# One store for five groups, and a last group in 12 KB runs: a batched matmul on one core

## The chip, the core and the metric

The kernel runs on one core of a Trainium2 chip. The core has a matrix engine (PE, with its weight loads PEld), a vector engine (DVE), a scalar engine (ACT), POOL, which does nothing here, and SP, which issues the transfers. All transfers between the chip's DRAM and the on-chip buffers run on 16 DMA engines, and one transfer is spread over all 16. The metric is device time in microseconds (us). The kernel before takes 134.25 us, the median of four runs (134.11 to 134.53).

## The reference

```
x: (32, 256, 512) float32      y: (32, 512, 384) float32
out = einsum('bij,bjk->bik', x, y)  as float32
```

There are 32 independent products of a 256x512 matrix with a 512x384 one. Inputs are 41.94 MB, outputs 12.58 MB.

## The kernel before

Four batches make a group, so there are eight groups, 0 to 7. A group's x, y and outputs lie on all 128 partitions, 32 partitions for each of its four batches. For x, a partition holds eight rows of 512 (16 KB, one run in DRAM); for y, sixteen rows of 384 (24 KB, one run). The outputs of a group take 12 KB per partition, eight rows of 384.

Each group goes through steps, each named by a letter with the group's number. `x` and `y` are the loads (lines 89 and 98). `T` casts x to float16 and transposes it in blocks of 32 by 32 on DVE (lines 108 and 115). `R` casts y to float16 on DVE (line 121). `M` is 128 matmuls (line 140): first the 64 of half `e` = 0, then the 64 of `e` = 1; within a half, four row strips of the matrix engine work for the four batches `g`. Each pair `(e, g)` has a bank of PSUM, the matmuls' output memory, and these are all eight banks. `C` and `D` copy the banks to the output tile (line 161): `C` is ACT's share and `D` DVE's, chosen by `on_vector`. `S` stores a group's output tile (line 168).

The order of the work is written out by hand in the string `PLAN`; each engine, and SP for the transfers, keeps that order. The stores of groups 0 to 4 stand after the last load, `y7`. Those of groups 5, 6 and 7 stand at the end.

How the rows of a group are dealt to partitions is decided by `width(n)`. For groups 0 to 5 it is 32: a copy moves 32 partitions by 384, a bank takes four copies, and a partition ends with eight consecutive rows of the output, one run of 12,288 B in DRAM. For groups 6 and 7 it is 64: a copy moves 64 partitions, a bank takes two, and a partition ends with two runs of 6,144 B that are 786,432 B apart in DRAM. `width` is used in the transpose, the copies and the store, which must agree.

Of the copies, DVE takes the last bank of groups 0 to 5, none of group 6, and the odd `g` of group 7; ACT takes the rest. So of the 16 copies of group 7 each of the two takes eight.

Buffers: x and y have two each. The output pool has five, for groups 0 to 4. Groups 5 and 6 put their outputs into x buffers that have been read; group 7 takes an output buffer again, the one that group 0 used, and so comes after store 0.

Of the kernel before, what the change touches and what calls it, by code (L numbers as in the profile page):

```python
# [1 line left out]

# [4 lines left out]


MM_DT = mybir.dt.float16
F32 = mybir.dt.float32  # L10
P = 128


Q = 4
STEP = 4
O_BUFS = 5
WIDE_GROUPS = 6

O_IN_X = (5, 6)

PLAN = """
y0 x0 y1 x1
R0 T0 M0 C0 x2 y2
R1 T1 D0 M1 C1 x3
T2 D1 R2 M2 C2 x4 y3
T3 D2 R3 M3 C3 x5 y4
T4 D3 R4 M4 C4 x6 y5  # L30
T5 x7 y6 D4 R5 T6 M5 C5 y7 S0 S1 S2 S3 S4
D5 R6 T7 M6 C6
R7 M7 C7 D7 S5 S6 S7
"""


@with_exitstack
def kernel(
    ctx: ExitStack,
    tc: tile.TileContext,  # L40
    x: bass.AP,
    y: bass.AP,
    out: bass.AP,
):
    nc = tc.nc

    B, I, J = x.shape
    _, _, K = y.shape

    PQ = P // Q  # L50
    R = I // PQ
    T = J // PQ
    TW = T // 2
    NE = I // P
    N = B // Q

    x_pool = ctx.enter_context(tc.tile_pool(name="x_pool", bufs=2))
    y_pool = ctx.enter_context(tc.tile_pool(name="y_pool", bufs=2))
    xr_pool = ctx.enter_context(tc.tile_pool(name="xr_pool", bufs=1))
    xt_pool = ctx.enter_context(tc.tile_pool(name="xt_pool", bufs=3))  # L60
    yr_pool = ctx.enter_context(tc.tile_pool(name="yr_pool", bufs=2))
    o_pool = ctx.enter_context(tc.tile_pool(name="o_pool", bufs=O_BUFS))
    psum_pool = ctx.enter_context(
        tc.tile_pool(name="psum", bufs=1, space=bass.MemoryType.PSUM)
    )

    keep = tc.keep_in_program_order

    bank = {
        (e, g): psum_pool.tile([P, K], F32, name=f"o_ps_{e}_{g}") for e in range(NE) for g in range(Q)  # L70
    }

    x_of, y_of, xt_of, yr_of, ps_of, o_of = {}, {}, {}, {}, {}, {}

    def width(n):
        return PQ if n < WIDE_GROUPS else 2 * PQ

    def on_vector(n, e, g):
        if n < WIDE_GROUPS:
            return (e, g) == (NE - 1, Q - 1)
        return n == N - 1 and g % 2 == 1

    def load_x(n):
        x_of[n] = x_pool.tile([P, R, J], F32, name="x_sb")
        keep(
            nc.sync.dma_start(
                out=x_of[n],  # L90
                in_=x[n * Q : (n + 1) * Q].rearrange("g (p r) j -> (g p) r j", r=R),
            )
        )

    def load_y(n):
        y_of[n] = y_pool.tile([P, T, K], F32, name="y_sb")
        keep(
            nc.sync.dma_start(  # L98
                out=y_of[n],
                in_=y[n * Q : (n + 1) * Q].rearrange("g (q t) k -> (g q) t k", t=T),  # L100
            )
        )

    def transpose_x(n):


        x_r = xr_pool.tile([P, R, J], MM_DT, name="x_r")
        keep(nc.vector.tensor_copy(x_r, x_of.pop(n)))  # L108
        xt_of[n] = xt_pool.tile([P, NE, TW, P], F32, name="xt_sb")
        b = width(n) // PQ  # L110
        src = x_r.bitcast(F32).rearrange("p (b h e) (q t) -> p b e t h q", b=b, e=NE, t=TW)
        dst = xt_of[n].rearrange("p e t (h s b) -> p b e t h s", s=PQ, b=b)
        for e in range(NE):
            for c in range(b):
                keep(nc.vector.transpose(dst[:, c, e], src[:, c, e]))  # L115

    def round_y(n):
        y_sb = y_of.pop(n)
        yr_of[n] = yr_pool.tile([P, T, K], MM_DT, name="y_r")
        for a in range(0, T, STEP):  # L120
            keep(nc.vector.tensor_copy(yr_of[n][:, a : a + STEP], y_sb[:, a : a + STEP]))  # L121

    def multiply(n):
        xt = xt_of.pop(n).bitcast(MM_DT).rearrange("p e t (m c) -> p e t m c", c=2)
        y_r = yr_of.pop(n)
        if n in O_IN_X:
            x_sb = x_pool.tile([P, R, J], F32, name="x_sb")
            o_of[n] = x_sb.rearrange("p r j -> p (r j)")[:, : R * K].rearrange(
                "p (r k) -> p r k", r=R
            )  # L130
        else:
            o_of[n] = o_pool.tile([P, R, K], F32, name="o_sb")
        for e in range(NE):
            for g in range(Q):
                ps_of[n, e, g] = bank[e, g]
            for t in range(T):
                for g in range(Q):
                    s = slice(g * PQ, (g + 1) * PQ)
                    keep(
                        nc.tensor.matmul(  # L140
                            ps_of[n, e, g],
                            xt[s, e, t // 2, :, t % 2],
                            y_r[s, t],
                            start=(t == 0),
                            stop=(t == T - 1),
                        )
                    )

    def collect(n, vector):
        w = width(n)  # L150
        per = P // w
        copy = nc.vector.tensor_copy if vector else nc.scalar.copy
        o = o_of[n].rearrange("p (u f) k -> p u f k", u=Q // per)
        for e in range(NE):
            for g in range(Q):
                if on_vector(n, e, g) != vector:
                    continue
                ps = ps_of.pop((n, e, g))
                a = g % per * w
                for h in range(per):  # L160
                    keep(copy(o[a : a + w, g // per, h * NE + e], ps[h * w : (h + 1) * w]))  # L161

    def store(n):
        w = width(n)
        per = P // w
        dst = out[n * Q : (n + 1) * Q].rearrange("(u g) (s f) k -> (g s) u f k", g=per, s=w)
        keep(
            nc.sync.dma_start(
                out=dst, in_=o_of.pop(n).rearrange("p (u f) k -> p u f k", u=Q // per)
            )  # L170
        )

    parts = {
        "x": load_x,
        "y": load_y,
        "T": transpose_x,
        "R": round_y,
        "M": multiply,
        "C": lambda n: collect(n, False),
        "D": lambda n: collect(n, True),  # L180
        "S": store,
    }
    for step in PLAN.split():
        parts[step[0]](int(step[1:]))


# [1 line left out]
_INS = ['x', 'y']  # L188
_OUTS = [((32, 256, 384), 'float32')]


# [23 lines left out]
```

## Time and profile before

| what | us |
|---|---|
| median of four runs | 134.25 |
| the profiled execution, its own time | 134.11 |
| its span, first to last instruction | 132.3 |
| DVE busy | 95.8 |
| ACT busy | 91.5 |
| PE busy | 58.9 |
| DMA queue q1, share of 16 engines' span | 97.2% |
| a copy on ACT, 32x384 / 64x384 | 0.469 / 0.473 |
| a copy on DVE, 32x384 / 64x384 | 0.556 / 0.556 |

A page of the profile shows one execution. Its second part cuts the span into 40 equal slices; a digit is the busy share of an engine in a slice in tenths (9 is 90% or more), and the DMA row is the mean busy share of the 16 DMA engines. The timeline lists instructions in order of time: start, length, engine, line, operation, output and input, count, and in brackets the idle time before and what ended it. A table of stretches gives, for each window, the busy time of each engine, the clock granted to the matrix engine, the DMA share and the rate in GB/s. The trace also keeps a record of every DMA packet (start, length, size) and the moment at which each of the 16 engines reports that its part of a transfer has landed; durations of packets and landings of single stores are read from these.

### The profile page before, as it was taken

Reading aid. Unit: us, or ns where it says so; the run is one execution under the profiler, and the core shown is the slowest. Engines: PE = TensorE matmul, PEld = TensorE weight load, DVE = VectorE, ACT = ScalarE, POOL = GpSimd, SP = SyncE. Lnnn points to the kernel's source line nnn. Section 1 sums busy time; section 2 is a strip of 40 time slices with the busy share of each in tenths; the row PEclk is TensorE's granted clock in tenths of the full one; section 3 lists DMA queues with packets and bytes.
Section 4 is the critical chain, followed back from the end, with each engine's and each line's share of the span. In section 5 each row is a group of like instructions: output and inputs, shape, how many; then the busy total and the mean of one; then the engine's idle time right before and its main releaser. Section 6 shows DMA issues by size and latency. Waiting matters only on the chain.

```text
span 132.3 us, 2431 instructions
## 1 busy us (share of the span) xinstructions
PE 58.9 (44%) x1024; PEld 33.3 (25%) x1024; DVE 95.8 (72%) x92; ACT 91.5 (69%) x193; POOL 0.2 (0%) x4
## 2 busy tenths in 40 slices
PE   0000008951956095708581668067705867750000
PEld 0000004420534043404350335033502454430000
DVE  0007696959999999879979995999699997642000
ACT  3000000299999999999999999999999999970000
POOL 0000000000000000000000000000000000000000
PEclk9999999999599959995899689977997799998555
DMA  5999999999999999999999999999999999999993
GB/s 134 446 416 421 458 416 419 446 421 448 438 406 426 421 441 436 419 411 463 409 421 431 443 423 409 421 456 438 409 443 386 431 430 414 435 421 427 409 425 165
DMA packets 3723, 54.68 MB, mean 413 GB/s; under 512 B 384, under 2 KB 384, under 8 KB 896
## 3 DMA queue, kind: packets, MB, share of 16 engines
q1 hardware_dynamic: 3712, 54.53, 97.2%
q8 instruction: 8, 0.13, 0.4%
q14 instruction: 3, 0.02, 0.0%
HBM read 41.94 MB, written 12.58 MB: 412 GB/s over the span
## 4 chain that ended last, share of the span: by engine, by line
ACT 63%; DMA 11%; PE 8%; DVE 4%; issue 3%; DVEq 1%; SPq 0%; ACTq 0%
ACT o_sb L161 49%; ACT x_sb L161 14%; DMA x_sb<-in_x_dram 11%; PE o_ps L140 8%; DVE x_r L108 2%; DVE xt_sb L115 2%; DVE o_sb L161 1%; DVEq L210 1%; SPq L98 0%; ACTq L161 0%
## 5 line engine op out<-in xcount | busy, mean ns | idle before, releaser
L161 ACT COPY o_sb<-o_ps 32x384 f32<-32x384 f32 (+1 forms) x148 | 69.5, 470 | 26.4 <-PE o_ps L140 24.3
L140 PE MATMUL o_ps<-y_r,xt_sb 32*128 32x384 f16 x1024 | 58.9, 381 | 58.7 <-DVE xt_sb L115 24.3
L140 PEld LDWEIGHTS <-xt_sb 32*128 32x128 f16 x1024 | 33.3, 108 | 83.8 <-DVE xt_sb L115 24.6
L121 DVE CAST y_r<-y_sb 128x1536 f16<-128x1536 f32 x32 | 28.5, 953 | 12.8 <-DMA y_sb<-in_y_dram 12.7
L115 DVE STREAM_TRANSPOSE xt_sb<-x_r 128x1024 f32<-128x1024 f32 (+1 forms) x20 | 31.7, 1635 | 0.3
L161 ACT COPY x_sb<-o_ps 32x384 f32<-32x384 f32 (+1 forms) x44 | 20.7, 471 | 0.7
L161 DVE COPY o_sb<-o_ps 32x384 f32<-32x384 f32 (+1 forms) x28 | 15.6, 556 | 6.7 <-PE o_ps L140 4.6
L108 DVE CAST x_r<-x_sb 128x4096 f16<-128x4096 f32 x8 | 18.3, 2289 | 2.7 <-DMA x_sb<-in_x_dram 2.7
L161 DVE COPY x_sb<-o_ps 32x384 f32<-32x384 f32 x4 | 2.2, 556 | 1.4 <-PE o_ps L140 1.4
L161 ACT ACT_TABLE_LOAD x1 | 1.3, 1283 | 0.7 <-PEq L199 0.7
L199 POOL MEMSET const-bfloat16-1.0<- 128x1 bf16 x1 | 0.1, 101 | 0.0
L199 POOL MEMSET const-uint8-127<- 128x1 uint8 x1 | 0.1, 101 | 0.0
L199 POOL MEMSET const-float32-0.0<- 128x1 f32 x1 | 0.1, 98 | 0.2 <-issue 0.2
L199 POOL MEMSET const-float32-1.0<- 128x1 f32 x1 | 0.1, 98 | 0.0
## 6 DMA issues: line engine op xcount, KB each, us to landing
y_sb<-in_y_dram SPq DMA_DIRECT2D x8, 3072.0 KB, 18.6
x_sb<-in_x_dram SPq DMA_DIRECT2D x8, 2048.0 KB, 13.5
out_dram<-o_sb SPq DMA_DIRECT2D x6, 1536.0 KB, 21.8
out_dram<-x_sb SPq DMA_DIRECT2D x2, 1536.0 KB, 15.2
```

The lines of the kernel that those rows point to most:

```text
L108: keep(nc.vector.tensor_copy(x_r, x_of.pop(n)))
L115: keep(nc.vector.transpose(dst[:, c, e], src[:, c, e]))
L121: keep(nc.vector.tensor_copy(yr_of[n][:, a : a + STEP], y_sb[:, a : a + STEP]))
L140: nc.tensor.matmul(ps_of[n, e, g], xt[s, e, t // 2, :, t % 2], y_r[s, t], start=(t == 0), stop=(t == T - 1),)
L161: keep(copy(o[a : a + w, g // per, h * NE + e], ps[h * w : (h + 1) * w]))
L199: nc = _bacc.Bacc("TRN2", target_bir_lowering=False, num_devices=1)
L210: with _tile.TileContext(nc) as tc:
```

## The change

Three things are edited. First, the outputs of groups 0 to 4 lie in one tile, `o_all`, of 128 partitions by five groups by 12 KB, and one step `E0` stores it in one transfer, in the place of `S0` to `S4`. On the DRAM side a partition then has five runs of 12,288 B, 1,572,864 B apart. Second, `width(7)` becomes 32: group 7 is copied in 32 copies of 32x384, 16 on each of ACT and DVE, and stored in one run of 12,288 B per partition. Group 6 stays as it was. Third, group 7's outputs go into a y buffer, through the same helper `left_by` that now serves the x buffers.

```diff
+NARROW_GROUPS = (6,)
+O_IN_X = (5, 6)
+O_IN_Y = (7,)
 O_BUFS = 5
-WIDE_GROUPS = 6
-O_IN_X = (5, 6)
...
-T5 x7 y6 D4 R5 T6 M5 C5 y7 S0 S1 S2 S3 S4
+T5 x7 y6 D4 R5 T6 M5 C5 y7 E0
 D5 R6 T7 M6 C6
 R7 M7 C7 D7 S5 S6 S7
...
-    o_pool = ctx.enter_context(tc.tile_pool(name="o_pool", bufs=O_BUFS))
+    o_pool = ctx.enter_context(tc.tile_pool(name="o_pool", bufs=1))
...
+    o_all = o_pool.tile([P, O_BUFS, R, K], F32, name="o_sb")
...
     def width(n):
-        return PQ if n < WIDE_GROUPS else 2 * PQ
+        return 2 * PQ if n in NARROW_GROUPS else PQ

     def on_vector(n, e, g):
-        if n < WIDE_GROUPS:
-            return (e, g) == (NE - 1, Q - 1)
-        return n == N - 1 and g % 2 == 1
+        if n == N - 1:
+            return g % 2 == 1
+        return n not in NARROW_GROUPS and (e, g) == (NE - 1, Q - 1)
+
+    def left_by(tile_sb):
+        o = tile_sb.rearrange("p a b -> p (a b)")[:, : R * K]
+        return o.rearrange("p (r k) -> p r k", r=R)
...
         if n in O_IN_X:
-            x_sb = x_pool.tile([P, R, J], F32, name="x_sb")
-            o_of[n] = x_sb.rearrange("p r j -> p (r j)")[:, : R * K].rearrange(
-                "p (r k) -> p r k", r=R
-            )
+            o_of[n] = left_by(x_pool.tile([P, R, J], F32, name="x_sb"))
+        elif n in O_IN_Y:
+            o_of[n] = left_by(y_pool.tile([P, T, K], F32, name="y_sb"))
         else:
-            o_of[n] = o_pool.tile([P, R, K], F32, name="o_sb")
+            o_of[n] = o_all[:, n]
...
+    def store_all(n):
+        dst = out[n * Q : (n + O_BUFS) * Q].rearrange("(c g) (s f) k -> (g s) c f k", g=Q, s=PQ)
+        keep(nc.sync.dma_start(out=dst, in_=o_all))
...
+        "E": store_all,
```

## The prediction

> **What bounds the kernel now.** Start with the page's second part, the span in 40 slices, and compare the engines' rows with the DMA row.
>
> ```profile
> DVE  0007696959999999879979995999699997642000
> ACT  3000000299999999999999999999999999970000
> DMA  5999999999999999999999999999999999999993
> q1 hardware_dynamic: 3712, 54.53, 97.2%
> ```
>
> The DMA row is at 9 from the second slice to the last but one; ACT is as full only from 25 to 119 us, and nothing but DMA runs in the last four slices. The one queue that carries loads and stores (q1) keeps the 16 DMA engines busy for 97.2% of the span. The page's fourth part, the chain, says "ACT 63%", but the chain follows engine instructions only: its last pieces are copies of group 7 that end at 119.8 us, 12.5 us before the end. So ask next what stands between 119.8 and 132.3: the timeline from 113 us, and the landings of the last store.
>
> ```profile
> 113.60 2.27 DVE L161 COPY o_sb<-o_ps 64x384 f32<-64x384 f32 x4 [1.79 <-ACT x_sb L161]
> 114.77 1.93 ACT L161 COPY o_sb<-o_ps 64x384 f32<-64x384 f32 x4
> 114.79 2.75 PE L140 MATMUL o_ps<-y_r,xt_sb 32*128 32x384 f16 x61 [0.66 <-ACT x_sb L161]
> 117.44 1.93 ACT L161 COPY o_sb<-o_ps 64x384 f32<-64x384 f32 x4 [0.75 <-PE o_ps L140]
> 117.55 2.27 DVE L161 COPY o_sb<-o_ps 64x384 f32<-64x384 f32 x4 [1.68 <-PE o_ps L140]
> 119.88 0.38 SPq L168 DMA_DIRECT2D out_dram<-o_sb  x1
> ```
>
> ```profile
> DMA to landing us min/median/max: 11.6/11.6/11.6
> ```
>
> The last store (S7) is issued at 119.88 and lands 11.6 us later, at 131.5; its own 1.57 MB need only 3.7 us of 16 engines. The other 8 us it stands behind older stores in the queue. The landing records of the trace give the queue's order (last of 16 engines, us): y7 102.31, S0 105.95, S1 109.58, S2 113.25, S3 116.88, S4 120.75, S5 124.20, S6 127.86, S7 131.50. Each step is 3.45 to 3.87 us. The third view is a table of stretches; the last two columns are DMA share and GB/s:
>
> ```profile
> 16.00:94.00 78.00, 43.04 (x722) 23.92 (x726) 71.29 (x63) 66.38 (x142) 0.00 (x0) 0.89 1.00 428
> 103.00:120.00 17.00, 11.48 (x233) 6.96 (x225) 13.22 (x17) 15.12 (x33) 0.00 (x0) 0.96 1.01 425
> 126.00:129.00 3.00, 0.00 (x0) 0.00 (x0) 0.00 (x0) 0.00 (x0) 0.00 (x0) 0.50 1.02 426
> ```
>
> Loads (to 94 us), stores in 12 KB runs (103 to 120) and stores in 6 KB runs (126 to 129) move at the same 425 to 428 GB/s, without a hole. The time is one uninterrupted DMA queue, from the first packet at 1.74 us to the last landing at 131.50, plus 0.8 us to the end of the span; the profiled execution took 134.11 us, its span 132.33, so 1.78 lie outside. That execution was the fastest of the four; the median is 134.25, 0.14 above it. A change counts here only if it shortens what the DMA engines do or opens a hole in their queue. A difference from no change can be told from about 0.3% of the time, 0.40 us.
>
> **The change part by part.**
>
> *Five stores become one (E0).* Bytes and data packets stay: 128 partitions by 5 runs of 12,288 B, 40 packets per DMA engine. The trace's packets of 12,288 B take 460 ns (median of 768), so 18.4 us per engine, before and after. What goes is four completion packets per engine (4 B, 9 ns each in the packet records): 4 x 9 = 36 ns. Is there a hidden price per store? From y7's landing to S4's is 18.44 us for five stores, and 5 x (8 x 460 + 9) ns = 18.45 us, so nothing is left over.
>
> [...]
>
> *E0 is issued later.* S0 was issued at 88.90 us; E0 waits for all of groups 0 to 4, that is for ACT's last copy of group 4, and S4, with the same wait, was issued at 93.34. E0 takes that place. The work that hides this is y6 and y7, still in the queue: the first DMA engine is done with y7 at 100.31 (first of its 16 landings). From issue to first packet the trace has one undisturbed row, the first load: issued at 0.73, packets begin at 1.74 on the first engine and 2.38 on the last. So E0's packets can begin near 93.34 + 1.0 = 94.4, 5.9 us before they are wanted. If setting up 640 runs stretches the 0.64 us of spread fivefold, 3.2 us of the cover are used. Cost 0; without the cover it would be 1.0 to 4.3 us. Behind E0 on SP stand S5, S6 and S7, issued at 106.91, 114.77 and 119.88, so SP is free long before.
>
> *E0's order.* An engine now takes a partition's five runs, 1,572,864 B apart in DRAM, before the next partition. No row shows this. The nearest is S6 and S7: two 6,144 B runs per partition, 786,432 B apart; all 512 of them took exactly 234 ns, 468 ns for 12,288 B against 460. If the 8 ns came from the jump and not from the shorter run, E0 would pay 40 x 8 = 0.32 us per engine. A worse bound is the loads: 200 of the 1,024 packets of y took longer than the median, by 72 ns on average; 40 x 0.2 x 72 = 0.58 us. A gain bound: 38 of the 768 stores were slower than 460 ns, which costs 0.15 us per engine; E0 could lose these. The worst: every packet as the mean of the 38 stores that were slow, 65 ns over, 40 x 65 = 2.6 us. I take 0, since the S6 rows, the only ones with jumps, are flat to the nanosecond, and two packet starts in place of one can be the whole of the 8 ns; ends -0.15 and +2.6, of which I hold up to +0.58 likely.
>
> [...]
>
> *Group 7 in 12 KB runs.* S7's 16 packets per engine of 234 ns become 8 of 460: 3,744 - 3,680 = 64 ns less, on the path. Group 6 keeps its form.
>
> *Group 7's copies double.* For each bank four copies of 32 partitions replace two of 64. Width costs nothing in the rows (ACT 470 ns for 32x384, 473 for 64x384; DVE 556 for both), so twice the copies is twice the time. DVE: 8 copies after the first half of the matmuls, from 113.60 at 0.567 us each (2.27/4) to 118.14, then 8 more, already ready, to 122.67. ACT: from 114.77, when it has finished group 6, 16 at 0.483 (1.93/4) to 122.50. Nothing is queued behind them on either engine; only S7 waits. S7 goes out at 122.74 instead of 119.88, 2.86 us later. Its packets could start at 122.74 + 1.01 = 123.75; the first DMA engine is done with S6 at 125.91. Cover left: 2.2 us on the first engine, 3.1 on the slowest (127.86 - 0.36 from last packet to landing, against 122.74 + 1.65). Cost 0 on the path.
>
> *Group 7's buffer.* Before, it took the buffer of group 0 and so had to wait for S0, landed at 105.95; the first copy is at 113.60, 7.6 us later: that wait cost nothing. The y buffer was last read by DVE in R6, done at about 102. Gain 0. It is needed only because E0, landing near 120.7, would otherwise be late for 113.60.
>
> *Instructions.* SP issues four fewer DMAs (0.4 us each, hidden). ACT and DVE get eight copies more each; instruction packets share the DMA engines (8 KB took 0.31 to 0.33 us, 16 KB about 1.0). One more of them would cost one engine 0.3 to 1.0 us, at the end only if it is the slowest. I take none; ends 0 and 1.0.
>
> Sum: -0.04 - 0.06 = -0.10 us. On the profiled execution: 134.11 - 0.10 = 134.01; on the median: **134.15 us**, less than can be told from no change.
>
> **Rivals.**
>
> *Late S7 (slower).* If group 7's copies did not run side by side on ACT and DVE, 16 x 0.483 + 16 x 0.567 = 16.8 us from 113.60 end at 130.4, the store starts on the last engine 1.65 later and takes 3.68 + 0.36: landing 136.1, so 134.25 + 4.6 = 138.8. It decides from an issue of S7 after 125.85. Against it: both engines write one tile at the same time in the rows above (114.77 to 115.87), which also speaks against waits between the writers of the one large tile of groups 0 to 4. Chance 0.05.
>
> *E0's packets slower.* By the bounds above +0.32 to +0.58, with the sum's -0.10 134.5 to 134.75, and at the far end of 2.6 us 136.75. It passes 134.65 from 0.50 us, 12.5 ns a packet. For it: no row has the step. Against it: the flat 234 ns. Chance of passing 134.65: 0.12.
>
> *One more instruction packet on the slowest engine.* +0.3 to +1.0: up to 135.1. Chance of passing 134.65: 0.05.
>
> *A more even end (faster).* S7's 16 landings go from 129.60 to 131.50, mean 130.75. Which engine is last follows from which got the slow and the instruction packets. With fewer completions and another order the ends could move together; all of it would be -0.75, so 133.4 to 133.8. Against it: nothing in the change balances engines. Chance 0.23.
>
> **How the numbers follow.** No change that can be told: 0.55; faster 0.23; slower 0.05 + 0.12 + 0.05 = 0.22. The likeliest case's own range is 133.85 to 134.65. The range takes in most of the even end below and of the slower packets above: 133.6 to 134.95; outside stay the late S7 (0.05), the far parts of the others (about 0.12).
>
> **What the profile after would show.** q1 with 3,520 packets (3,712 less 64 completions less 128 runs); one store of 7.9 MB at about 93.3 us, landing near 120.7; S7 issued near 122.7 and landing after about 8.7 us; DMA still at 9 throughout; copies of group 7 as 32x384, 16 on each engine. Wrong would be: a dip in the DMA row near 100 us (E0 late) or 126 us (S7 late), or 12,288 B packets above 460 ns between 102 and 121 us.

## The result and the profile after

The changed kernel takes 134.52 us (median of 45 runs) against 134.31 us for the kernel before, measured beside it (68 runs): ratio 1.0019, interval 1.0015 to 1.0024, so 0.20 to 0.32 us slower. The forecast was 134.15 us, 0.10 us faster. The time lies in the stated range and inside what was called no change, 0.40 us, but with this many runs a shift can be told from zero, and its sign is the other one.

In the DMA engines the page shows what was forecast. These are lines of its second and third parts for the changed kernel (of the queue: packets, MB, share of the 16 engines):

```profile
DMA  4999999999999999999999999999999999999992
q1 hardware_dynamic: 3520, 54.53, 96.8%
```

The DMA row is still full from the second slice to the last but one, and the queue has the 3,520 packets that were expected. The stretch in which the one large store runs moves 425 GB/s, as the five stores did:

```profile
103.00:120.00 17.00, 11.89 (x229) 6.87 (x219) 14.87 (x20) 16.46 (x36) 0.00 (x0) 0.90 1.01 425
```

The timeline of the changed kernel from 92 us on shows the steps of the prediction; the large store in this view is the line with `o_sb`, at L181:

```profile
92.86 0.40 SPq L181 DMA_DIRECT2D out_dram<-o_sb  x1
...
113.13 9.07 DVE L167 COPY y_sb<-o_ps 32x384 f32<-32x384 f32 x16 [1.93 <-PE o_ps L146]
...
114.28 7.68 ACT L167 COPY y_sb<-o_ps 32x384 f32<-32x384 f32 x16
...
122.26 0.33 SPq L174 DMA_DIRECT2D out_dram<-y_sb  x1
```

The large store goes out at 92.86 us (forecast 93.3) and lands at 120.68 (120.7). Group 7's 16 and 16 copies run side by side, and its store goes out at 122.26 (122.74). The last landing is at 131.65 us, against 131.50 before.

The span, though, grew from 132.33 to 132.73, by 0.40. So 0.26 us of it lie behind the last landing: from there to the end of the span it is 0.82 us before and 1.08 after. Two views show what stands there. First the waits of SP's queue from 119 us on, in the kernel before and then in the changed one; L210 and L221 are the end of the program, and the columns are the time waited, how often, and the longest:

```profile
SPq L210 <- DMA out_dram<-x_sb: 7.0, 2, 3.6
SPq L168 <- DVE o_sb L161: 4.7, 1, 4.7
SPq L210 <- DMA out_dram<-o_sb: 4.0, 2, 3.6
```

```profile
SPq L221 <- DMA out_dram<-y_sb: 9.1, 1, 9.1
```

Before, the program's end waits four times, in turn for S4, S5, S6 and S7, as they land. After, it waits once, 9.1 us, for the very last store. The second view is the line of these wait instructions, again before and then after (durations in ns, then first and last start in us):

```profile
L210 SPq EVENT_SEMAPHORE  x7: 17/28/28, 120.3 to 132.3; - x7
```

```profile
L221 SPq EVENT_SEMAPHORE  x7: 17/28/28, 131.7 to 132.7; - x7
```

Both have seven wait instructions, the first five for the transfers. Before, the five start at 120.30, 120.76, 124.22, 127.88 and 131.52, so that only the fifth stands behind the last landing. After, all five do. The trace's records of the five in the changed kernel (start, length in ns, semaphores waited for; the last landing is at 131.65):

```
131.663 28 Sync EVENT_SEMAPHORE $S[104]>= $S[102]>=
131.732 28 Sync EVENT_SEMAPHORE $S[105]>= $S[100]>=
131.793 28 Sync EVENT_SEMAPHORE $S[107]>= $S[99]>=
131.858 28 Sync EVENT_SEMAPHORE $S[108]>= $S[101]>=
131.919 28 Sync EVENT_SEMAPHORE $S[109]>= $S[103]>=
```

The records of the transfers say which semaphore each one signals. Eight completion semaphores are used in turn: 99, 100, 102, 104, 105, 107, 108, 109. Before there are 24 transfers, so the last one signals 109, which is waited for last. With one store in the place of five there are 20, and the last signals 104, which is in the first wait. The other four instructions, each about 64 ns after the one ahead (131.919 - 131.663 = 0.256 us in all), find their transfers long done but still have to be gone through, with nothing left to hide them. That this is the whole loss is called theory T in the experiments. It has two rivals there: the order of the large store's runs costs time (P), or the later issue of the last store does (C).

### The profile page after: what moved, and what is told of

The parts are those of the page before. It is cut to its first block, busy times and chain, and to the rows that moved or that the text cites. A ratio compares the mean times of both kernels' runs of the same rounds, so it can differ in the third digit from the quotient of the medians.

```text
span 132.7 us, 2440 instructions
## 1 busy us (share of the span) xinstructions
PE 64.0 (48%) x1024; PEld 35.8 (27%) x1024; DVE 100.1 (75%) x98; ACT 95.2 (72%) x201; POOL 0.2 (0%) x4
## 3 DMA queue, kind: packets, MB, share of 16 engines
q1 hardware_dynamic: 3520, 54.53, 96.8%
## 4 chain that ended last, share of the span: by engine, by line
ACT 64%; DMA 11%; DVE 6%; PE 6%; issue 4%; DVEq 0%; SPq 0%; ACTq 0%
ACT o_sb L167 49%; ACT x_sb L167 15%; DMA x_sb<-in_x_dram 11%; PE o_ps L146 6%; DVE y_sb L167 3%; DVE x_r L115 2%; DVE xt_sb L122 2%; DVEq L221 0%; SPq L105 0%; ACTq L167 0%
## 5 line engine op out<-in xcount | busy, mean ns | idle before, releaser
L146 PE MATMUL o_ps<-y_r,xt_sb 32*128 32x384 f16 x1024 | 64.0, 406 | 53.0 <-DVE xt_sb L122 25.0
L167 ACT COPY o_sb<-o_ps 32x384 f32<-32x384 f32 x140 | 65.7, 470 | 25.1 <-PE o_ps L146 23.0
L146 PEld LDWEIGHTS <-xt_sb 32*128 32x128 f16 x1024 | 35.8, 113 | 80.9 <-DVE xt_sb L122 25.4
L167 DVE COPY o_sb<-o_ps 32x384 f32<-32x384 f32 x20 | 11.1, 556 | 2.0 <-PE o_ps L146 1.7
L167 DVE COPY y_sb<-o_ps 32x384 f32<-32x384 f32 x16 | 8.9, 554 | 2.1 <-PE o_ps L146 1.9
L167 ACT COPY y_sb<-o_ps 32x384 f32<-32x384 f32 x16 | 7.5, 469 | 0.2
L210 POOL MEMSET const-bfloat16-1.0<- 128x1 bf16 x1 | 0.1, 101 | 0.0
L210 POOL MEMSET const-uint8-127<- 128x1 uint8 x1 | 0.1, 101 | 0.0
L210 POOL MEMSET const-float32-0.0<- 128x1 f32 x1 | 0.1, 98 | 0.2 <-issue 0.2
L210 POOL MEMSET const-float32-1.0<- 128x1 f32 x1 | 0.1, 98 | 0.0
```

The costliest lines, as they stand in the source:

```text
L146: nc.tensor.matmul(ps_of[n, e, g], xt[s, e, t // 2, :, t % 2], y_r[s, t], start=(t == 0), stop=(t == T - 1),)
L210: nc = _bacc.Bacc("TRN2", target_bir_lowering=False, num_devices=1)
```

## The experiments

**Five stores out of the one tile.** The large store alone is undone; group 7 stays in 12 KB runs.

```diff
     def store_all(n):
-        dst = out[n * Q : (n + O_BUFS) * Q].rearrange("(c g) (s f) k -> (g s) c f k", g=Q, s=PQ)
-        keep(nc.sync.dma_start(out=dst, in_=o_all))
+        for c in range(n, n + O_BUFS):
+            store(c)
```

> The changed kernel with its one large store taken apart again into five, in the old place, out of the same tile; group 7 stays in 12 KB runs. Theory T (tail): eight completion semaphores are used in turn and SP waits for them in a fixed order at the end; with 24 transfers the last store signals the one that is waited for last, with 20 it signals one with four more wait instructions of 0.064 us behind it. Here there are 24, so the stretch from last landing to end of span is 0.83 us as before, and the time is that of before less 0.06 for the shorter packets of group 7: ratio 0.9995. Theory P (the order of the large store costs): also back at the time of before, but with the tail of the changed kernel unchanged at about 1.08 us and the last landing earlier. Theory C (the late last store costs): no better than the changed kernel, ratio 1.002.

Ratio 0.9995 (0.9986 to 1.0003); the stretch behind the last landing is 0.82 us, theory T's value. Theory C falls: the last store here goes out as late as in the changed kernel (123.05 us) and costs nothing. P expected the gain in the last landing; that is at 131.68, no earlier than in the changed kernel.

**The large store alone.** Group 7 goes back to 6 KB runs.

```diff
-NARROW_GROUPS = (6,)
+NARROW_GROUPS = (6, 7)
```

> The large store alone: group 7 goes back to 6 KB runs and half as many copies, its outputs stay in the y buffer. Theory T: 20 transfers, tail 1.08 us, 134.31 + 0.26 - 0.04 = 134.53, ratio 1.0016. Theory P: ratio 1.002 too, with the last landing 0.2 to 0.3 us later than before and a tail of 0.83. Theory C: ratio 1.000.

Ratio 1.0015 (1.0006 to 1.0023). The last landing is at 131.52, as before (131.50); the stretch behind it is 1.08 us. Its line of waits has the form of the changed kernel:

```profile
L221 SPq EVENT_SEMAPHORE  x7: 17/28/28, 131.5 to 132.5; - x7
```

So the large store alone brings the loss, and the DMA engines end no later than before.

**The same order of runs in five pieces.** This was to keep the order and have 24 transfers.

```diff
-        keep(nc.sync.dma_start(out=dst, in_=o_all))
+        for lo, hi in ((0, 32), (32, 64), (64, 96), (96, 112), (112, 128)):
+            keep(nc.sync.dma_start(out=dst[lo:hi], in_=o_all[lo:hi]))
```

> The large store cut by partitions into five pieces (32, 32, 32, 16, 16 partitions): every partition still writes its five runs one after another, 1.57 MB apart, but there are 24 transfers. Theory T: tail 0.83 us, ratio 0.9995. Theory P: the order is that of the changed kernel, so ratio 1.002. Theory C: ratio 1.002.

Ratio 1.1799 (1.1778 to 1.1821): all three theories missed by far, since the edit brought a cost of its own. The stretches show it; the last two columns are DMA share and GB/s:

```profile
90.00:102.00 12.00, 6.86 (x116) 3.69 (x112) 10.50 (x14) 11.63 (x26) 0.00 (x0) 0.78 0.97 414
102.00:110.00 8.00, 7.32 (x120) 4.05 (x113) 7.97 (x6) 7.74 (x17) 0.00 (x0) 0.70 1.03 244
110.00:120.00 10.00, 6.62 (x121) 3.89 (x123) 6.03 (x10) 8.25 (x18) 0.00 (x0) 0.85 1.00 231
120.00:130.00 10.00, 0.95 (x12) 0.14 (x1) 4.43 (x8) 3.75 (x8) 0.00 (x0) 0.50 1.04 167
```

From 102 us on, when the pieces run, the DMA engines are as busy as ever but move little more than half of the 425 GB/s of whole stores, and from 120 us on less. The records have packets of 12,288 B that typically take 947 to 948 ns (between 104 and 115 us) in place of 460. As a test of the order the run is lost. The one reading that stands is the stretch behind the last landing, 0.82 us with 24 transfers, as T has it.

**Before, with 28 transfers by halves.** Stores 0 to 3 are each cut in two by partitions.

```diff
+HALVED = (0, 1, 2, 3)
...
-        keep(
-            nc.sync.dma_start(
-                out=dst, in_=o_of.pop(n).rearrange("p (u f) k -> p u f k", u=Q // per)
-            )
-        )
+        o = o_of.pop(n).rearrange("p (u f) k -> p u f k", u=Q // per)
+        cuts = (0, 64, P) if n in HALVED else (0, P)
+        for lo, hi in zip(cuts, cuts[1:]):
+            keep(nc.sync.dma_start(out=dst[lo:hi], in_=o[lo:hi]))
```

> The kernel before with stores 0 to 3 each cut into two halves of 64 partitions: 28 transfers, no large store, group 7 as before. Theory T: the last store signals the same semaphore as in the changed kernel, tail 1.08 us, and four more completions of 9 ns: 134.31 + 0.26 + 0.04 = 134.61, ratio 1.0022. Theories P and C: nothing of theirs is in it, ratio 1.0003 for the completions alone.

Ratio 1.0391 (1.0357 to 1.0424), again a cost of the cut itself. The stretch behind the last landing is 1.08 us with 28 transfers, T's value. As a test by time this run is lost too. Both ideas were then tried again with nothing cut by partitions.

**The changed kernel with 24 transfers.** Four small loads ahead of the large store; their values are not used.

```diff
+    n_pool = ctx.enter_context(tc.tile_pool(name="n_pool", bufs=1))
+    n_sb = n_pool.tile([P, 4, P], F32, name="n_sb")
+
+    def small(n):
+        keep(nc.sync.dma_start(out=n_sb[:16, n], in_=x[n, :16, :P]))
...
+        "n": small,
...
-T5 x7 y6 D4 R5 T6 M5 C5 y7 E0
+T5 x7 y6 D4 R5 T6 M5 C5 y7 n0 n1 n2 n3 E0
```

> The changed kernel with four small loads (16 partitions by 512 B, into a tile that nobody reads) put ahead of the large store, so that there are 24 transfers and the last store signals the semaphore that is waited for last. The large store itself is whole and keeps all 128 partitions. Theory T (tail): tail 0.82 us instead of 1.08; the small loads cost each DMA engine four packets and four completions, some 0.15 us at most; against before -0.10 + 0.15 at most, ratio 0.9992 to 1.0005, and 0.1 to 0.26 us below the changed kernel beside it. Theory P (the order or size of the large store costs) and theory C (the later last store costs): ratio 1.002 to 1.003.

Ratio 1.0002 (0.9991 to 1.0013), 0.16 us below the changed kernel's median beside it, with four transfers more to do. The line of waits starts at 122.0 again, and behind the last landing are 0.82 us:

```profile
L228 SPq EVENT_SEMAPHORE  x7: 17/28/28, 122.0 to 132.4; - x7
```

The large store is whole here, with its order, and the last store goes out at 121.59. With P or C the loss would have stayed.

**The kernel before with 28 transfers.** The same four loads ahead of S0.

```diff
-T5 x7 y6 D4 R5 T6 M5 C5 y7 S0 S1 S2 S3 S4
+T5 x7 y6 D4 R5 T6 M5 C5 y7 n0 n1 n2 n3 S0 S1 S2 S3 S4
```

> The kernel before with the same four small loads ahead of store 0: 28 transfers, five separate stores, group 7 as before. Theory T: the last store signals the semaphore that the changed kernel's signals, four wait instructions follow: tail 1.08 us, with the small loads +0.26 to +0.41 us, ratio 1.0019 to 1.003. Theories P and C: +0.15 us at most, ratio 1.000 to 1.001.

Ratio 1.0030 (1.0017 to 1.0044), stretch 1.08 us. The four loads have a small cost of their own, the same in both kernels: from the mean landing of y7 to that of the last store it is about 0.10 us more with them (29.56 against 29.46 for the changed kernel beside it, 29.63 against 29.52 for the kernel before). With the tail, theory T has -0.26 + 0.10 = -0.16 us for the run above, against the changed kernel, and +0.26 + 0.10 = +0.36 us for this one, against the kernel before; the medians measured beside each other differ by -0.16 and +0.34. The same loads make the one kernel faster and the other slower: what decides is which semaphore the last store signals. The waits here are those of the changed kernel:

```profile
SPq L217 <- DMA out_dram<-o_sb: 11.4, 1, 11.4
```

**The last store later, to the point of decision.** ACT makes 24 of group 7's 32 copies.

```diff
         if n == N - 1:
-            return g % 2 == 1
+            return g == 1
```

> The changed kernel, but ACT makes 24 of group 7's 32 copies and DVE eight: the last copy ends near 114.3 + 24 x 0.48 = 125.8 us and the last store is issued there, at the prediction's point of decision (125.85). Theory T with the cover as the prediction has it: the fastest DMA engines stand idle for about 1 us, the slowest hardly at all; last landing 131.6 to 131.9, ratio 1.0015 to 1.004. If the cover is smaller than was worked out (theory C), 0.5 us or more is lost against the changed kernel: ratio 1.006 or more.

Ratio 1.0020 (1.0009 to 1.0031); the changed kernel beside it had 1.0013. The store goes out at 126.15, 3.9 us later than in the first profile of the changed kernel, and lands at 131.90. The cover was there. On average the 16 engines land 0.5 us later than in the changed kernel beside it (131.20 against 130.73), but the last of them only 0.17 us later, and the last one sets the time.

**The last store past the point.** ACT makes all 32.

```diff
         if n == N - 1:
-            return g % 2 == 1
+            return False
```

> The changed kernel, but ACT makes all 32 copies of group 7: the last ends near 114.3 + 32 x 0.48 = 129.7 us, past the prediction's point of decision (125.85), and the last store is issued there into an empty queue. With the prediction's 1.65 us to the last engine's first packet, 3.68 for eight packets and 0.36 to landing: landing near 135.4 instead of 131.65, time 134.52 + 3.75 = 138.3, ratio 1.029. If the cover did not exist at all (theory C), the 7.4 us by which the store is later than in the changed kernel would all be paid: ratio 1.056. If it were larger than worked out, less than 1.02.

Ratio 1.0268 (1.022 to 1.0316). The timeline and the stretches of this run:

```profile
114.31 15.41 ACT L167 COPY y_sb<-o_ps 32x384 f32<-32x384 f32 x32
...
129.75 0.33 SPq L174 DMA_DIRECT2D out_dram<-y_sb  x1
```

```profile
122.00:126.00 4.00, 0.00 (x0) 0.00 (x0) 0.00 (x0) 3.89 (x10) 0.00 (x0) 0.50 0.98 410
126.00:129.00 3.00, 0.00 (x0) 0.00 (x0) 0.00 (x0) 2.93 (x7) 0.00 (x0) 0.50 0.22 92
129.00:131.00 2.00, 0.00 (x0) 0.00 (x0) 0.00 (x0) 0.71 (x2) 0.00 (x0) 0.50 0.23 98
```

Here is the hole that a late store makes: the DMA share falls from 0.98 to 0.22 between 126 and 131 us. The store lands at 134.84, 5.09 us after its issue, where 5.69 were forecast. The term that was too long is the start: with nothing else in the queue the 16 engines have their first packets 0.83 to 0.98 us after issue, not 1.01 to 1.65, the values that the first load had lent.

**The changed kernel once more.**

> The changed kernel once more, beside the three others. Theory T: tail +0.26, less work for the DMA engines -0.10: ratio 1.0012; the first comparison had 1.0019 (1.0015 to 1.0024).

Ratio 1.0013 (1.0003 to 1.0022), the stretch behind the last landing 1.08 us.

## Why the prediction was wrong

*The step that failed* is the first part's "plus 0.8 us to the end of the span". It was taken over as a constant and had no term in the sum. It holds five wait instructions of the program's end, and whether they lie under the last store or behind it depends on the number of transfers, which the change lowers from 24 to 20. The missing term is +0.256 us. With it the sum is -0.10 + 0.256 = +0.16 us, ratio 1.0012; measured were 1.0013 (1.0003 to 1.0022) and 1.0019 (1.0015 to 1.0024). The working followed the transfers that go into completions and issue times, but not into the waits for them.

*Five stores become one: -0.04.* Size and place were right, as far as single executions show it. From the mean landing of y7 to that of the last store it is 29.52 us before, 29.49 with the large store alone, 29.48 with the 12 KB runs alone and 29.45 with both: -0.03, -0.04 and -0.07, where -0.04, -0.06 and -0.10 were forecast. The second profile of the changed kernel has 29.46. The last of the 16 landings does not show the gain; its delay of 0.15 us in the changed kernel's first profile is of a size that is there already in the fifth transfer (33.76 against 33.55), long before anything that was edited.

*E0's issue and order: 0.* Right. The store went out 7.3 us before its first DMA engine was free (100.18), and its 40 packets per engine were no slower: packets of 12,288 B take 460 ns (median) and 462.6 (mean) after, 460 and 463.2 before. E0's steps of 1,572,864 B within a partition cost nothing that these packets show.

*Group 7's copies, store and buffer: 0 and -0.06.* Right. T7 changed with `width(7)` too, which the working left out: two transposes of 1,024 columns in place of four of 512, 3.94 us against 4.07 on DVE, hidden.

*The rivals.* None of them was it. The late S7 has nearly the price and the point that were worked out: issued at 126.15 it costs nothing that can be told beside the changed kernel (point of decision: 125.85), and at 129.75 the last landing is 3.3 us later than before (134.84 against 131.50), where the prediction's terms give 3.9. Slower packets and one more instruction packet did not come (three packets on q14 and eight on q8, as before). A more even end did not come either: the last store's landings spread over 2.19 us, against 1.90.

*Slips in the working that change nothing.* The last four slices do not hold DMA alone: DVE's digit there is 2 in the first of them, for copies that end at 119.8 us. Of the 768 stores 57, not 38, took longer than 460 ns, by 43 ns on average, and of the y packets 491, not 200, longer than their median, by 30; the costs of 0.15 and 0.58 us stay, and the worst bound of 2.6 us becomes 1.7. Without the cover, E0 would cost up to 1.0 + 3.2 = 4.2 us, not 4.3.

*What stays open.* The first comparison's interval starts at 1.0015, above the 1.0012 of the sum. The difference, 0.04 to 0.16 us, is not explained; the second comparison has no need of it.

No version here clearly beats the kernel before. Group 7 in 12 KB runs with five stores, at 0.9995 (0.9986 to 1.0003), is the best.

## What to carry to other kernels

Where a full DMA queue sets the time, as here, count what stands behind the last landing too: read the waits of the issuing queue at the program's end, before and after, and see whether the last transfer is the one that is waited for last. Merging transfers that already ran back to back saved only their completions here (9 ns each per engine), and it lost more than that, because the number of transfers decides which semaphore the last one signals; here 24 was a good number and 20 and 28 were not. The cover that was worked out from when the queue runs dry held in the one place where it was tried; delaying the transfer step by step is a way to measure it.

## What the runs showed that was not expected

Stores that cover a part of the partitions were expensive here. In the pieces of 32 partitions a packet of 12,288 B typically took 947 to 948 ns, and in the run with pieces single ones took up to 2.9 us, against 460 for whole stores; the rate fell from 425 to 231-244 GB/s, and to 167 between 120 and 130 us. The 16 engines also came apart: in that run the last store's landings spread over 11.1 us (144.44 to 155.57). That was never caught up: the spread was 11.1 us at the end of the last piece (133.42 to 144.57) already, three whole stores earlier. Halves of 64 partitions left the typical packet at 460 ns (mean 502), but the last store's landings spread over 9.3 us in the profiled execution; that one took 141.95 us, while the 3.9% stand for 139.6. Why the engines come apart was not tried.

The two cuts do not slow the packets alike. In the pieces of 32 partitions 948 ns is 2.06 times 460; with the halves the typical packet took 460 ns, and the stretch from 102 to 110 us still moved 400 GB/s. Whether lower and upper halves that follow each other in the queue shared the time was not tried, so no run here shows a cause.
